# A fused encoder block on one core: row squares, row scaling, output casts and weight casts queued behind the newest operation of their engine, and token tiles requested earlier

## The chip, the cores and the metric

The kernel runs on one core of a Trainium2 chip. Five engines of that core work side by side, each on its own list of instructions in order: TensorE (PE in the profile) multiplies, VectorE (DVE) does two-input elementwise work, ScalarE (ACT) does copies, squares, exponentials and scaling, GpSimd (POOL) does powers and issues some transfers, and SyncE (SP) issues most transfers between the device memory and the on-chip memory. An instruction that needs another engine's result waits for it, and everything behind it on the same engine waits too.

The metric is the device time of one execution in microseconds (us), lower is better. The kernel before takes 2262.73 us, the median of three runs (2262.56, 2262.73 and 2266.06).

## The reference

One transformer layer over 16 meta tokens and 2048 tokens of width 1024, all in float32: a shared input projection, grouped-query attention with 4 query heads and 2 key/value heads, a Fourier mixing of the other half of the channels, an output projection, and an MLP with squared ReLU.

```python
def reference(x, meta_tokens, g_mix, w_in, g_q, g_k, w_fourier, g_attn_out, g_fourier_out, w_out,
              g_mlp, w_up, w_down, g_final):
    h = concat([meta_tokens, x], axis=1)                      # 2064 rows of 1024
    proj = rms_norm(h, g_mix) @ w_in
    q, k, v, u = split(proj)                                  # 512, 256, 256, 512 columns
    q = axial_rope(rms_norm(q, g_q)); k = axial_rope(rms_norm(k, g_k))
    attn = softmax(q k^T / sqrt(128)) v                       # 4 heads of 128, 2 kv heads
    four = real(fft2(u over tokens and 128 channels)) @ w_fourier
    h = h + concat([rms_norm(attn, g_attn_out), rms_norm(four, g_fourier_out)]) @ w_out
    m = rms_norm(h, g_mlp)
    h = h + square(relu(m @ w_up)) @ w_down
    return rms_norm(h, g_final)[:, 16:]
```

## The kernel before

A float32 product is made of three matmuls (`mm3`, lines L81 to L83): each operand is split into a high part, which ACT casts (L71, or L74 with a scale), and a low part, which DVE subtracts (L72, or L75 with a scale). The words "cast" and "low part" below mean these two.

**Stages.** Up to about 230 us the tokens are normalised, transposed and projected, in eight steps j of 256 tokens. Then come the Fourier stage and its output projection, and beside them the attention, which goes on to about 1000 us. The attention's own output projection (`out_a`) and the transposing of its rows (`flip`) run beside the last attention units. From about 1042 us to the end TensorE multiplies for the MLP.

**Tokens.** `load_x(j)` asks on SP for the two tiles x_j_0 and x_j_1 (128 rows of 1024); the tag "x" has three buffers. `prep(j)` squares and sums each row (L249, names jk), has POOL raise the mean to the power -1/2 (L194, names rs_x), scales the row (L254), transposes it on TensorE (L294, names pt), splits it into hth and htl, and stores both parts to ht_d on SP (L304). At its end it asks for both tiles of step j + 1. Projections of q, k and v follow (names pq, pkv), and transposes of q (ptq, L452).

**Weights.** `weight_parts` (L469 to L478) loads eight blocks of w_out (names wf), casts them with a scale (L74 and L75) and stores the parts; each block is loaded, and cast one step later, beside the steps of `prep`. The tag "wf" has one buffer, so that a load waits until the block before it has been stored.

**Attention.** Sixteen units u, each of 512 queries (two heads of 256 tokens) against 17 key tiles. TensorE makes scores s, and ACT copies them out of two rotating banks into S (L829); DVE takes a running maximum M (L835 and L824), subtracts a row (L889), ACT takes the exponential (L890), DVE adds to a sum (L896), and TensorE multiplies by v (L898). `finish(u)` copies the unit's output O, waits for a transfer of the inverse sums (rb), 12 steps later multiplies by it (L917), casts it (ohl, L71), stores it, and squares it (L931).

**Rows behind the attention.** For block b (0 to 3) `out_a(b)` works through four tiles t of 128 rows. For each half of a row TensorE makes poa, DVE adds it to the residual (L1122, names h), and ACT squares the half (L1123, names hj). After the second half DVE sums, POOL takes the power (L194, names rs_m), the row is stored, and `scale_row` scales the row tile before (L1134). `flip(b)` scales the last tile and transposes the rows on TensorE (L1146, names pmt), ACT evacuating each with a scale (L1148, names mt). `mix` and `beside` interleave the generators: a step of `out_a`, a step of the block before's `flip`, and then as many attention steps as fall to it.

**What sets the order.** The program text gives each engine a first order, and a scheduler then settles the order of every engine when the program is built. `tc.issue_after(i)` ties the instructions inside its block, those on the engine of i, to stand behind i; `ins_of` takes the instruction out of a call's result. In the kernel before, the multiplication by rb (L917) is tied to the newest sum (`held["sub"]`); the squares, the scaling, the output cast and the weight casts are not tied to anything.

Of the kernel before, what the change touches and what calls it, by code (L numbers as in the profile page):

```python
# [11 lines left out]
F32 = mybir.dt.float32  # L12
# [45 lines left out]
def f32v(ap):  # L58
    return ap.bitcast(F32)


class Split:
# [5 lines left out]
    def __call__(self, hi, lo, src, scale=None):  # L68
        nc = self.nc
        if scale is None:  # L70
            self.high = nc.scalar.copy(hi, src)  # L71
            self.low = nc.vector.tensor_tensor(lo, src, f32v(hi), op=ALU.subtract)  # L72
        else:
            nc.scalar.activation(hi, src, AF.Copy, scale=scale)  # L74
            self.low = nc.vector.scalar_tensor_tensor(lo, src, scale, f32v(hi), op0=ALU.mult, op1=ALU.subtract)  # L75


# [8 lines left out]
def ins_of(x):  # L86
    return getattr(x, "ins", x)
# [49 lines left out]
def encoder_block(ctx: ExitStack, tc: tile.TileContext, x, meta, w_in, w_f,  # L137
# [26 lines left out]

    xs = {}

    def load_x(j):
        rows = META if j == "m" else P
        for a in range(1 if j == "m" else 2):
            t = tp.tile([P, D], F32, name=f"x_{j}_{a}", tag="x", bufs=3)  # L170
            src = meta if j == "m" else x[(2 * j + a) * P:(2 * j + a + 1) * P, :]
            nc.sync.dma_start(t[:rows], src)
            xs[j, a] = t
# [103 lines left out]

    def prep(j):

        if j == 0:  # L280
            norm_first()
        else:
            for a in range(2):
                norm_x(j, a)
        if j == LAST:
            norm_x("m", 0)
        hT[j] = []
        for kk in range(KT // 2):
            yield
            ps = tbank(f"pt_{j}_{kk}")  # L290
            for i in range(2):
                for a in range(2):
                    k = 2 * kk + i
                    nc.tensor.transpose(ps[:, i * 256 + a * P:i * 256 + (a + 1) * P],  # L294
                                        xs[j, a][:, k * P:(k + 1) * P], ident)
            hi, lo = (t2k(f"ht{e}_{j}_{kk}", [P, 2, 256 + (META if j == LAST else 0)]) for e in "hl")
            split(hi[:, :, :256], lo[:, :, :256], ps.rearrange("p (i n) -> p i n", i=2))
            if (j, kk) == (0, 0):
                early["h"], early["l"] = ins_of(split.high), ins_of(split.low)
            hT[j].append((hi, lo))  # L300
            if 0 < j < LAST:
                for e, t in enumerate((hi, lo)):
                    c = slice((j - 1) % 2 * 256, (j - 1) % 2 * 256 + 256)
                    nc.sync.dma_start(ht_d[(j - 1) // 2][:, 2 * kk:2 * kk + 2, e, c], f32v(t))  # L304
        if j == LAST:
            pm = tbank("pt_m", (P, KT, META))
            for k in range(KT):
                nc.tensor.transpose(pm[:, k, :], xs["m", 0][:META, k * P:(k + 1) * P], ident[:META, :META])
            for kk, (hi, lo) in enumerate(hT[j]):
                split(hi[:, :, 256:], lo[:, :, 256:], pm[:, 2 * kk:2 * kk + 2, :])  # L310
        if 0 < j < LAST:
            load_x(j + 1)
        if j == LAST - 1:
            load_x("m")

    def h_op(j, k, sl):
        if j == "m":
# [151 lines left out]
    def weight_parts():  # L469

        for (k, h), dst in wf_d.items():
            t = wpp.tile([P, 2, 512], R32, name=f"wf{k}_{h}", tag="wf")
            raw = f32v(t[:, 1])
            nc.sync.dma_start(raw, w_out[512 + k * P:512 + (k + 1) * P, h * 512:(h + 1) * 512])
            yield
            split(t[:, 0], t[:, 1], raw, c_fo(k))
            nc.sync.dma_start(dst, f32v(t))
            yield  # L478

# [287 lines left out]
    def a_operand(b, heads):  # L767
# [5 lines left out]
                    nc.sync.dma_start(f32v(A[:, e, k]), o_d[b][:, e, k])  # L773
        return AT[b]

    def attention():

        units = [(b0 + qh, g) for i, (b0, n) in enumerate(BLOCKS)
# [3 lines left out]
        def load_q(u):  # L782
# [1 line left out]
            q = ap.tile([P, 2, 2, 256], R32, name=f"q_{u}", tag="q", bufs=2)  # L784
            nc.gpsimd.dma_start(q, q_d[b][:, :, 2 * g:2 * g + 2])
            return q.rearrange("p l h n -> p l (h n)")

        held = {}

        def start(u, q=None):  # L790
            q = load_q(u) if q is None else q
# [70 lines left out]
        def softmax(u, i):  # L862
# [24 lines left out]
            if i % 2 == 0:  # L887
                mb = s["mb"].rearrange("p (o n) -> p o n", o=1).broadcast_to([P, 2, 512])
                nc.vector.tensor_tensor(S, S, mb, op=ALU.subtract)  # L889
                nc.scalar.activation(p, S, AF.Exp, scale=ISQ)  # L890
                return
            v = vt[j // 2]
            if j == 1:
# [6 lines left out]
        def finish(u):  # L900
# [8 lines left out]
            if u < len(l_d):  # L909
                nc.sync.dma_start(l_d[u], rl)  # L910
                rb = ap2.tile([P, 512], F32, name=f"rb_{u}", tag="rb", bufs=1)
                nc.sync.dma_start(rb, l_d[u].rearrange("(o p) a -> o (p a)", o=1).broadcast_to([P, 512]))
                for _ in range(12):
                    yield
                v = O.rearrange("p (a e) -> p a e", a=4)
                with tc.issue_after(held["sub"]):
                    nc.vector.tensor_tensor(v, v, rb.rearrange("p (e a) -> p a e", a=4), op=ALU.mult)  # L917
            else:
                yield
                nc.vector.tensor_tensor(O, O, rows_to_cols(rl, f"l{u}"), op=ALU.mult)  # L920
            c = slice(b % 2 * 256, b % 2 * 256 + 256)
            if u >= len(units) - 2:
                A = a_operand(3, (2, 3))
                split(A[:, 0, 2 * g:2 * g + 2, c], A[:, 1, 2 * g:2 * g + 2, c], O.rearrange("p (h n) -> p h n", h=2))
            else:
                hl = ap2.tile([P, 2, 512], R32, name=f"ohl_{u}", tag="ohl", bufs=1)
                split(hl[:, 0], hl[:, 1], O)
                for e in range(2):
                    nc.sync.dma_start(o_d[b // 2][:, e, 2 * g:2 * g + 2, c],
                                      f32v(hl[:, e]).rearrange("p (h n) -> p h n", h=2))  # L930
# [165 lines left out]
    def out_a(b):  # L1096
# [14 lines left out]
        ra = rstd_of(mp, ss[:, :T], T, 512, "a")  # L1111
        A = a_operand(b, range(NQ))
        MS[b] = ms = []
        for t in range(T):
            ts = slice(t * P, (t + 1) * P)
            sums = mp.tile([P, 2], F32, name=f"hss_{b}_{t}", tag="hss", bufs=8)
            for half in range(2):
                c = slice(half * 512, (half + 1) * 512)
                ps = bank(f"poa_{b}_{half}_{t}")
                for k in range(NQ):  # L1120
                    mm3(nc, ps, (A[:, 0, k, ts], A[:, 1, k, ts]), WO[k, half], k == 0, k == NQ - 1)
                nc.vector.scalar_tensor_tensor(hs[t][:, c], ps, ra[:, t:t + 1], hs[t][:, c], op0=ALU.mult, op1=ALU.add)  # L1122
                nc.scalar.activation(a_tile(f"hj_{b}_{t}_{half}"), hs[t][:, c], AF.Square,  # L1123
                                     accum_out=sums[:, half:half + 1])
                yield
            sm = mp.tile([P, 1], F32, name=f"hsm_{b}_{t}", tag="hsm", bufs=4)
            nc.vector.tensor_tensor(sm, sums[:, 0:1], sums[:, 1:2], op=ALU.add)
            ms.append(rstd_of(mp, sm, 1, D, ("m", "m2")[b % 2]))
            nc.sync.dma_start(h_d[2 * b0 + t], hs[t])
            if t:  # L1130
                scale_row(b, t - 1)

    def scale_row(b, t):
        nc.scalar.activation(H[b][t], H[b][t], AF.Copy, scale=MS[b][t])  # L1134

    def flip(b):

        if b < 2:
            yield
        scale_row(b, 3)  # L1140
        yield
        hs = H.pop(b)
# [672 lines left out]
```

## Time and profile before

| | |
|---|---|
| median of three runs | 2262.73 us |
| the profiled execution | 2263.3 us |
| its span in the trace | 2261.5 us, so 1.8 us lie around the span |
| granted TensorE clock, mean | 0.996 |
| ACT busy | 1171.4 us, 52% of the span |
| POOL busy | 254.4 us, 11% of the span |
| moved by DMA | 408.08 MB, mean 180 GB/s |

A row of the profile names the engine, the source line, the operation, the output tile and the input tiles (without their numbers), the count, the busy time, and in brackets how long the engine sat idle before it and which engine's instruction ended that idle time. A row of times of start and duration belongs to the view in order of time. A row of a stretch "820.00:860.00" gives, for each engine, the busy time and in brackets the instructions, then the granted TensorE clock (1.00 is full speed) and the share of the DMA engines. Matmul durations are modelled and overlap: at full rate a matmul of 512 columns is listed with some 390 ns while one starts every 227 ns or so.

### The profile page before, as it was taken

To read this page: it belongs to the slowest core of one execution; us is meant where nothing else is said; L and a number is where in the kernel's file an instruction comes from. 1 tells how busy PE (TensorE), PEld (TensorE's weight loads), DVE (VectorE), ACT (ScalarE), POOL (GpSimd) and SP (SyncE) were. 2 spreads that over 40 slices of the span, in tenths; PEclk is the share of its full clock that TensorE was granted. 3 is DMA by queue.
4 is the path that set the end of the run, shared out by engine and by line. 5 is a ranking of instruction groups with operands and counts; after the bars stand their busy time and mean duration, and the time that the engine had idled before them with its cause. 6 is when DMAs were issued, how large, how long until landed. Compare 5 with 4: busy or idle time off the path is not lost.

```text
span 2261.5 us, 27682 instructions
## 1 busy us (share of the span) xinstructions
PE 2227.5 (98%) x9890; PEld 1755.5 (78%) x9890; DVE 1688.2 (75%) x2260; ACT 1171.4 (52%) x1991; POOL 254.4 (11%) x301
## 2 busy tenths in 40 slices
PE   9899999999999999999999999999999999999998
PEld 7788867777777666667888888888888888888887
DVE  6555299999888888988667668788765656786795
ACT  6454255556555656667655554334455555543343
POOL 2232200112332112100000020000110000200000
PEclk9999999999999999999999999999999999999999
DMA  7774743445346424456777577445594444954442
GB/s 267 236 235 136 253 134 90 82 116 167 121 146 200 160 75 133 136 202 246 261 240 241 184 275 249 131 131 171 179 370 172 152 151 154 343 177 152 131 138 84
DMA packets 219914, 408.08 MB, mean 180 GB/s; under 512 B 19568, under 2 KB 97776, under 8 KB 218112
## 3 DMA queue, kind: packets, MB, share of 16 engines
q1 hardware_dynamic: 192000, 343.64, 45.3%
q0 software_dynamic: 27632, 62.41, 9.0%
q8 instruction: 78, 1.28, 0.2%
q14 instruction: 60, 0.49, 0.1%
q10 hardware_dynamic: 144, 0.26, 0.0%
HBM read 260.16 MB, written 146.08 MB: 180 GB/s over the span
## 4 chain that ended last, share of the span: by engine, by line
PE 76%; DVE 10%; issue 4%; DMA 3%; ACT 3%; POOL 1%; SPq 0%; POOLq 0%; DVEq 0%; ACTq 0%
PE o L898 6%; PE dx L83 5%; PE dx L82 5%; PE dx L81 5%; PE ux L83 4%; PE ux L81 4%; PE ux L82 4%; PE dy L83 4%; PE dy L82 4%; PE dy L81 4%; PE uy L83 3%; PE uy L81 3%; PE uy L82 3%; PE s L81 2%; PE s L83 2%
## 5 line engine op out<-in xcount | busy, mean ns | idle before, releaser
L71 ACT CAST ah<-a 128x1024 fp32r<-128x1024 f32 x108 | 112.9, 1050 | 261.4 <-PE dx L82 106.4
L898 PE MATMUL o<-S,vn 128*128 128x512 f32 x512 | 243.7, 597 | 0.1
L829 ACT COPY S<-s 128x512 f32<-128x512 f32 x256 | 147.8, 586 | 130.2 <-PE s L83 121.5
L82 PE MATMUL dx<-bl,ah 128*128 128x512 f32 x496 | 192.5, 388 | 0.0
L83 PE MATMUL dx<-bh,al 128*128 128x512 f32 x496 | 192.5, 388 | 0.0
L81 PE MATMUL dx<-bh,ah 128*128 128x512 f32 x496 | 192.5, 388 | 0.0
L83 PE MATMUL ux<-bf,wul 128*128 128x512 f32 x448 | 174.3, 389 | 0.7 <-DVE wul L72 0.7
L81 PE MATMUL ux<-bf,wuh 128*128 128x512 f32 x448 | 174.5, 389 | 0.0
L82 PE MATMUL ux<-bf,wuh 128*128 128x512 f32 x448 | 174.3, 389 | 0.0
L889 DVE TENSOR_TENSOR S<-S,mb 128x1024 f32<-128x1024 f32 x128 | 153.2, 1221 | 19.8 <-ACT mb L860 19.7
L81 PE MATMUL s<-q,kt 128*128 128x512 f32 (+1 forms) x272 | 151.2, 556 | 10.3 <-ACT S L829 8.8
L890 ACT ACTIVATE S<-S 128x1024 f32<-128x1024 f32 x128 | 134.8, 1064 | 47.9 <-DVE S L889 46.7
L72 DVE TENSOR_TENSOR al<-a,ah 128x1024 fp32r<-128x1024 f32 x108 | 131.0, 1219 | 33.3 <-ACT ah L71 33.0
L81 PE MATMUL dy<-bh,ah 128*128 128x512 f32 (+1 forms) x388 | 150.5, 388 | 0.0
L82 PE MATMUL dy<-bl,ah 128*128 128x512 f32 (+1 forms) x388 | 150.5, 388 | 0.0
L83 PE MATMUL dy<-bh,al 128*128 128x512 f32 (+1 forms) x388 | 150.5, 388 | 0.0
L898 PEld LDWEIGHTS o<-S,vn 128*128 128x128 f32 x512 | 93.6, 190 | 69.7 <-issue 58.5
L835 DVE TENSOR_TENSOR M<-M,S 128x1024 f32<-128x1024 f32 x96 | 117.1, 1220 | 17.1 <-ACT S L829 16.2
L81 PE MATMUL uy<-bf,wuh 128*128 128x512 f32 x320 | 124.9, 390 | 2.0 <-ACT wuh L71 2.0
L83 PE MATMUL uy<-bf,wul 128*128 128x512 f32 x320 | 124.7, 390 | 0.8 <-DVE wul L72 0.8
L82 PE MATMUL uy<-bf,wuh 128*128 128x512 f32 x320 | 124.7, 390 | 0.0
L1279 ACT ACTIVATE c<-c 128x512 f32<-128x512 f32 x96 | 60.5, 631 | 122.1 <-DVE c L1327 120.3
(330 smaller groups left out, 5589.0 us busy)
## 6 DMA issues: line engine op xcount, KB each, us to landing
a<-s_d SPq DMA_DIRECT2D x84, 512.0 KB, 3.9
R<-in_w_up_dram SPq DMA_DIRECT2D x32, 1024.0 KB, 5.5
s_d<-s SPq DMA_DIRECT2D x128, 256.0 KB, 2.1
s_d<-c SPq DMA_DIRECT2D x96, 256.0 KB, 2.7
d<-in_w_down_dram SPq DMA_DIRECT2D x48, 512.0 KB, 5.1
f_d<-lf SPq DMA_DIRECT2D x56, 256.0 KB, 3.1
bf<-f_d SPq DMA_DIRECT2D x7, 2048.0 KB, 13.2
hk<-ht_d SPq DMA_DIRECT2D x24, 512.0 KB, 4.9
```

Source lines behind the costliest of these rows:

```text
L71: self.high = nc.scalar.copy(hi, src)
L72: self.low = nc.vector.tensor_tensor(lo, src, f32v(hi), op=ALU.subtract)
L81: nc.tensor.matmul(out, a[0], b[0], start=first, stop=False, skip_group_check=chain)
L82: nc.tensor.matmul(out, a[0], b[1], start=False, stop=False, skip_group_check=chain)
L83: nc.tensor.matmul(out, a[1], b[0], start=False, stop=last, skip_group_check=chain)
L829: nc.scalar.copy(S[:, i % 2], ps)
L835: nc.vector.tensor_tensor(M, M, S, op=ALU.max)
L889: nc.vector.tensor_tensor(S, S, mb, op=ALU.subtract)
L890: nc.scalar.activation(p, S, AF.Exp, scale=ISQ)
L898: nc.tensor.matmul(s["O"], v[:, 2 * j % 4 + e], p[:, e], start=i + e == 1, stop=False)
L1279: nc.scalar.activation(dst, src, AF.Relu)
```

## The change

It has five parts.

1. `load_x` takes the tiles to load. At the start of `prep(j)` it asks for the first tile of step j + 1, and at its end for the second.
2. In `weight_parts` each load stands behind the newest store of ht on SP, and the cast and the low part stand behind the newest cast and the newest low part that went through the helper `split`.
3. In `out_a` the squares of a half, and the sum, the power, the store and the scaling of a row, are put into a list `late`, which is emptied one half later, behind the next half's matmuls (for the last block at once, as before). For blocks 0 to 2 the square and the scaling stand behind the newest exponential (`held["exp"]`).
4. `flip` of blocks 0 and 1 loses its first empty step.
5. In `finish` the multiplication by rb comes after 10 steps in place of 12, and the cast one step later, tied to the newest exponential.

```diff
@@ Split
-            nc.scalar.activation(hi, src, AF.Copy, scale=scale)
+            self.high = nc.scalar.activation(hi, src, AF.Copy, scale=scale)
@@ load_x
-    def load_x(j):
+    def load_x(j, tiles=(0, 1)):
...
-        for a in range(1 if j == "m" else 2):
+        for a in tiles:
@@ prep
+        if 0 < j < LAST:
+            load_x(j + 1, (0,))
...
-                    nc.sync.dma_start(ht_d[(j - 1) // 2][:, 2 * kk:2 * kk + 2, e, c], f32v(t))
+                    early["store"] = ins_of(nc.sync.dma_start(ht_d[(j - 1) // 2][:, 2 * kk:2 * kk + 2, e, c], f32v(t)))
...
-            load_x(j + 1)
+            load_x(j + 1, (1,))
@@ weight_parts
-            nc.sync.dma_start(raw, w_out[512 + k * P:512 + (k + 1) * P, h * 512:(h + 1) * 512])
+            with tc.issue_after(early["store"]):
+                nc.sync.dma_start(raw, w_out[512 + k * P:512 + (k + 1) * P, h * 512:(h + 1) * 512])
             yield
-            split(t[:, 0], t[:, 1], raw, c_fo(k))
+            with tc.issue_after(ins_of(split.high)), tc.issue_after(ins_of(split.low)):
+                split(t[:, 0], t[:, 1], raw, c_fo(k))
@@ softmax
-                nc.scalar.activation(p, S, AF.Exp, scale=ISQ)
+                held["exp"] = ins_of(nc.scalar.activation(p, S, AF.Exp, scale=ISQ))
@@ finish
-                for _ in range(12):
+                for _ in range(10):
                     yield
...
+                yield
...
-                split(hl[:, 0], hl[:, 1], O)
+                with tc.issue_after(held["exp"]):
+                    nc.scalar.copy(hl[:, 0], O)
+                nc.vector.tensor_tensor(hl[:, 1], O, f32v(hl[:, 0]), op=ALU.subtract)
@@ out_a
+        late = []
+
+        def square(t, half, sums):
+            with behind_exp(b):
+                nc.scalar.activation(a_tile(f"hj_{b}_{t}_{half}"), hs[t][:, half * 512:half * 512 + 512], AF.Square,
+                                     accum_out=sums[:, half:half + 1])
+
+        def row_end(t, sums):
+            sm = mp.tile([P, 1], F32, name=f"hsm_{b}_{t}", tag="hsm", bufs=4)
+            nc.vector.tensor_tensor(sm, sums[:, 0:1], sums[:, 1:2], op=ALU.add)
+            ms.append(rstd_of(mp, sm, 1, D, ("m", "m2")[b % 2]))
+            nc.sync.dma_start(h_d[2 * b0 + t], hs[t])
+            if t:
+                scale_row(b, t - 1)
+
+        def flush():
+            while late:
+                f, *args = late.pop(0)
+                f(*args)
...
+                flush()
                 nc.vector.scalar_tensor_tensor(hs[t][:, c], ps, ra[:, t:t + 1], hs[t][:, c], op0=ALU.mult, op1=ALU.add)
-                nc.scalar.activation(a_tile(f"hj_{b}_{t}_{half}"), hs[t][:, c], AF.Square,
-                                     accum_out=sums[:, half:half + 1])
+                late.append((square, t, half, sums))
+                if half:
+                    late.append((row_end, t, sums))
+                if b == 3:
+                    flush()
                 yield
-            sm = mp.tile([P, 1], F32, name=f"hsm_{b}_{t}", tag="hsm", bufs=4)
...
+        flush()
+
+    def behind_exp(b):
+        return tc.issue_after(held["exp"]) if b < 3 else nullcontext()

     def scale_row(b, t):
-        nc.scalar.activation(H[b][t], H[b][t], AF.Copy, scale=MS[b][t])
+        with behind_exp(b):
+            nc.scalar.activation(H[b][t], H[b][t], AF.Copy, scale=MS[b][t])
@@ flip
-        if b < 2:
-            yield
         scale_row(b, 3)
```

What the change moves on the engines is seen in the order of the built programs. The first place is SP in step j = 2, around the load of x_3_1 (names: hth_2_k and htl_2_k are the parts of the tokens of step 2, wf2_0 a block of the output weights, qt_2 transposed queries). Before:

```order
L477 DMA wf_d1_1_139<-wf1_1_1695 128x1024
L474 DMA wf2_0_1847<-in_w_out_dram 128x512
L304 DMA ht_d0_144<-hth_2_2_912 128x2x256
L304 DMA ht_d0_144<-htl_2_2_913 128x2x256
L456 DMA q_d1_106<-qt_2_923 1024x1x128
L304 DMA ht_d0_144<-hth_2_3_932 128x2x256
L304 DMA ht_d0_144<-htl_2_3_933 128x2x256
L172 DMA x_3_1_940<-in_x_dram 128x1024
```

The same place on SP in the changed kernel:

```order
L306 DMA ht_d0_144<-htl_2_1_848 128x2x256
L306 DMA ht_d0_144<-hth_2_2_914 128x2x256
L172 DMA x_3_1_940<-in_x_dram 128x1024
L306 DMA ht_d0_144<-htl_2_2_915 128x2x256
L458 DMA q_d1_106<-qt_2_925 1024x1x128
```

The load of x_3_1 stands behind the store of hth_2_2 in place of the store of htl_2_3, and the store and the load of weight blocks that stood ahead of it are gone from there (they follow in steps 3 to 6).

The second place is ACT around the scaling of row tile h_0_3, at the end of unit 11's exponentials (S_11_n) and among the copies of unit 12's scores (S_12_n). Before:

```order
L829 COPY S_12_10_7359<-s_12_10_7355 128x512
L829 COPY S_12_10_7359<-s_12_11_7363 128x512
L890 ACTIVATE S_11_12_7101<-S_11_12_7101 128x1024
L931 ACTIVATE O_10_7228<-O_10_7228 128x512
L1134 ACTIVATE h_0_3_6792<-h_0_3_6792,rs_m_7399 128x1024
L829 COPY S_12_12_7376<-s_12_12_7372 128x512
L829 COPY S_12_12_7376<-s_12_13_7380 128x512
L890 ACTIVATE S_11_14_7143<-S_11_14_7143 128x1024
```

The same place on ACT in the changed kernel:

```order
L833 COPY S_12_10_7357<-s_12_11_7361 128x512
L1164 ACTIVATE h_0_2_6790<-h_0_2_6790,rs_m_7285 128x1024
L894 ACTIVATE S_11_12_7099<-S_11_12_7099 128x1024
L833 COPY S_12_12_7374<-s_12_12_7370 128x512
L833 COPY S_12_12_7374<-s_12_13_7379 128x512
L894 ACTIVATE S_11_14_7150<-S_11_14_7150 128x1024
L1164 ACTIVATE h_0_3_6792<-h_0_3_6792,rs_m_7408 128x1024
L833 COPY S_12_14_7400<-s_12_14_7396 128x512
```

The scaling of h_0_3 now stands behind two copies and one exponential that stood behind it; the scaling of the tile before, h_0_2, has come to stand where h_0_3 was.

The third place is ACT around the scaling of h_1_0, among the exponentials of unit 12 and the copies of unit 13 (hj_1_1_0 is a square of the next row tile, mt_0_k an evacuation of block 0's transposes). Before:

```order
L829 COPY S_13_6_7588<-s_13_6_7584 128x512
L1134 ACTIVATE h_1_0_7403<-h_1_0_7403,rs_m2_7594 128x1024
L890 ACTIVATE S_12_6_7307<-S_12_6_7307 128x1024
L890 ACTIVATE S_12_8_7326<-S_12_8_7326 128x1024
L890 ACTIVATE S_12_10_7359<-S_12_10_7359 128x1024
L1123 ACTIVATE hj_1_1_0_7612,hss_1_1_7597<-h_1_1_7405 128x512
L1148 ACTIVATE mt_0_0_7619<-pmt_0_0_7614,cols_97 128x512
L829 COPY S_13_6_7588<-s_13_7_7624 128x512
L829 COPY S_13_8_7641<-s_13_8_7637 128x512
```

The same place on ACT in the changed kernel:

```order
L833 COPY S_13_6_7594<-s_13_6_7590 128x512
L894 ACTIVATE S_12_6_7305<-S_12_6_7305 128x1024
L894 ACTIVATE S_12_8_7324<-S_12_8_7324 128x1024
L894 ACTIVATE S_12_10_7357<-S_12_10_7357 128x1024
L1176 ACTIVATE mt_0_1_7625<-pmt_0_1_7620,cols_97 128x512
L833 COPY S_13_6_7594<-s_13_7_7630 128x512
L1125 ACTIVATE hj_1_1_0_7689,hss_1_1_7596<-h_1_1_7414 128x512
L894 ACTIVATE S_12_12_7374<-S_12_12_7374 128x1024
L833 COPY S_13_8_7647<-s_13_8_7643 128x512
L833 COPY S_13_8_7647<-s_13_9_7651 128x512
L1164 ACTIVATE h_1_0_7412<-h_1_0_7412,rs_m2_7616 128x1024
```

The scaling of h_1_0 has gone from ahead of three exponentials and two copies to behind them; the second copy of S_13_6 comes one square earlier.

More of the change, by code (lines that the diff above doesn't have):

```diff
@@ L311, in prep @@
         if 0 < j < LAST:
-            load_x(j + 1)
+            load_x(j + 1, (1,))
         if j == LAST - 1:
-            load_x("m")
+            load_x("m", (0,))
     def h_op(j, k, sl):
@@ L774, in a_operand @@
         return AT[b]
+    held = {}
     def attention():
@@ L786, in load_q @@
             return q.rearrange("p l h n -> p l (h n)")
-        held = {}
         def start(u, q=None):
@@ L1121, in out_a @@
                     mm3(nc, ps, (A[:, 0, k, ts], A[:, 1, k, ts]), WO[k, half], k == 0, k == NQ - 1)
+                flush()
                 nc.vector.scalar_tensor_tensor(hs[t][:, c], ps, ra[:, t:t + 1], hs[t][:, c], op0=ALU.mult, op1=ALU.add)
-                nc.scalar.activation(a_tile(f"hj_{b}_{t}_{half}"), hs[t][:, c], AF.Square,
-                                     accum_out=sums[:, half:half + 1])
-                yield
-            sm = mp.tile([P, 1], F32, name=f"hsm_{b}_{t}", tag="hsm", bufs=4)
[L1127 to L1131, printed above, removed]
+                late.append((square, t, half, sums))
[3 more added lines that the diff above has]
+                    flush()
+                yield
+        flush()
+    def behind_exp(b):
+        return tc.issue_after(held["exp"]) if b < 3 else nullcontext()
     def scale_row(b, t):
-        nc.scalar.activation(H[b][t], H[b][t], AF.Copy, scale=MS[b][t])
+        with behind_exp(b):
+            nc.scalar.activation(H[b][t], H[b][t], AF.Copy, scale=MS[b][t])
     def flip(b):
-        if b < 2:
-            yield
         scale_row(b, 3)
```

## The prediction

> **What bounds the kernel now.** I began with the busy shares of the page, then went to TensorE's own waits, then to stretches of time.
>
> ```profile
> span 2261.5 us, 27682 instructions
> PE 2227.5 (98%) x9890; PEld 1755.5 (78%) x9890; DVE 1688.2 (75%) x2260; ACT 1171.4 (52%) x1991; POOL 254.4 (11%) x301
> PE s L81 <- ACT S L829: 8.8, 6, 2.4
> PE pm_m L843 <- DVE M L824: 3.6, 5, 0.9
> PE pt L294 <- ACT x L254: 2.3, 1, 2.3
> PE ptq L452 <- ACT jk L249: 2.3, 1, 2.3
> PE uy L81 <- ACT wuh L71: 2.0, 1, 2.0
> PE pq L83 <- DVE htl L72: 1.7, 1, 1.7
> PE uy L83 <- DVE wul L72: 0.8, 1, 0.8
> 780.00:820.00 40.00, 38.14 (x144) 25.30 (x143) 36.02 (x42) 23.90 (x40) 4.88 (x3) 1.00 0.19 54
> 900.00:940.00 40.00, 37.37 (x154) 25.64 (x155) 32.74 (x40) 27.39 (x45) 5.30 (x8) 1.00 0.41 136
> 1042.00:2240.00 1198.00, 1196.62 (x5274) 989.27 (x5273) 862.64 (x1042) 578.86 (x806) 44.99 (x77) 1.00 0.57 195
> ```
>
> TensorE is the bound: 2227.5 of 2261.5 us. The change takes no matmul away, so it can save at most TensorE's idle time and what reduced clock follows it. The MLP stretch offers nothing (1196.62 of 1198 busy); everything lies ahead of 1042 us, and the waits above name the places (8.8 us in six waits for score copies, two waits of 2.3 us for a token tile). DVE, at 36.02 of 40 us in 780 to 820, is the next limit there.
>
> **The tokens (part 1).** SP, ACT, TensorE and the clock around the load of x_3_1:
>
> ```profile
> 75.03 0.59 ACT L71 CAST hth<-pt 128x512 fp32r<-128x512 f32 x1
> 78.09 0.35 SPq L474 DMA_DIRECT2D wf<-in_w_out_dram  x1
> 82.31 1.20 SPq L172 DMA_DIRECT2D x<-in_x_dram  x1
> DMA to landing us min/median/max: 3.5/4.7/6.3
> 88.17 0.60 ACT L249 ACTIVATE jk<-x 128x512 f32<-128x512 f32 x1 [3.57 <-DMA x<-in_x_dram]
> 90.62 1.15 ACT L254 ACTIVATE x<-x,rs_x 128x1024 f32<-128x1024 f32 x1 [0.86 <-POOL rs_x L194]
> 88.94 0.55 PE L452 MATMUL ptq<-ident,qn 128*128 128x128 f32 x3 [2.29 <-ACT jk L249]
> 91.82 0.90 PE L294 MATMUL pt<-ident,x 128*128 128x128 f32 x3 [2.33 <-ACT x L254]
> 92.00:95.50 3.50, 3.50 (x12) 2.92 (x13) 1.74 (x4) 1.36 (x5) 1.33 (x1) 0.59 0.46 133
> ```
>
> The load was issued at 82.31, ACT waited 3.57 us for it, and the squares, power and scaling took from 88.17 to 91.77. TensorE stood 2.29 + 2.33 us, and then ran 3.5 us at 0.59 of its clock, another 3.5 × 0.41 = 1.4: 6.0 us in all. In the new order the load stands right behind the store of hth_2_2, whose cast ended at 75.62, and no weight load (held until 78.09 by its buffer) is ahead. Issued at about 76, landed by 82.3 even at the longest 6.3, and scaled 3.6 later at 85.9, the tile is there before TensorE's first idle moment (88.94 − 2.29 = 86.65). Bounds: −6.0 and, if something else is late at once, 0. I take **−6.0**: the margin of 0.7 us holds with the slowest landing. Its cover gone, the price is the 6.0 again. The wait of 1.7 for htl may shrink with the weight cast gone from ACT's path; I count nothing.
>
> **The weight casts (part 2).** They are moved, not removed:
>
> ```profile
> L74 ACT ACTIVATE wf<-wf,cols x8: 722/724/747, 33.7 to 124.9; 128x512 fp32r<-128x512 f32 x8
> L75 DVE SCALAR_TENSOR_TENSOR wf<-wf,cols x8: 742/748/1225, 38.2 to 125.7; 128x512 fp32r<-128x512 f32 x8
> ```
>
> Eight of 0.72 us on ACT and 0.75 on DVE go to steps 3 to 6, the loads on SP behind the ht stores. At worst each delays a cast that TensorE awaits, 8 × 0.75 = +6.0; at best 0, since ACT's other waits there are long. I take +0.5, near the row: in that stage TensorE waited for DVE's token parts just once, 1.7 us.
>
> **Row scaling and squares (part 3).** The power on POOL, ACT and TensorE at three row tiles (h_1_0, h_0_3, h_1_2):
>
> ```profile
> L194 POOL TENSOR_TENSOR rs_m<-ms_m,mhalf x16: 547/1036/4870, 756.6 to 1029.5; 128x1 f32<-128x1 f32 x16
> 853.20 3.73 POOL L194 TENSOR_TENSOR rs_m<-ms_m,mhalf 128x1 f32<-128x1 f32 x1 [4.60 <-DVE ms_m L192]
> 853.03 3.48 DVE L889 TENSOR_TENSOR S<-S,mb 128x1024 f32<-128x1024 f32 x3
> 856.96 1.15 ACT L1134 ACTIVATE h<-h,rs_m 128x1024 f32<-128x1024 f32 x1 [3.28 <-POOL rs_m L194]
> 862.04 1.05 ACT L829 COPY S<-s 128x512 f32<-128x512 f32 x2
> 862.66 0.65 PE L81 MATMUL s<-q,kt 128*128 128x512 f32 x1 [2.42 <-ACT S L829]
> 862.50:866.00 3.50, 3.34 (x6) 2.02 (x7) 3.36 (x3) 2.14 (x4) 0.00 (x0) 0.55 0.20 75
> 827.79 0.50 PE L81 MATMUL s<-q,kt 128*128 128x512 f32 x1 [2.02 <-ACT S L829]
> 831.00:835.00 4.00, 4.00 (x11) 3.12 (x10) 2.09 (x3) 1.25 (x2) 1.76 (x1) 0.50 0.00 0
> 901.71 0.50 PE L81 MATMUL s<-q,kt 128*128 128x512 f32 x1 [2.08 <-ACT S L829]
> ```
>
> A power over 128 numbers takes 0.55 us at best and 3.73 here, just while DVE ran three two-input subtractions without a break (853.03 to 856.51). ACT stood 3.28 us in front of the scaling; the copies behind it came at 862.04, and TensorE, with two score banks, stood 2.42. In the new order the three exponentials and the copies go ahead of this scaling: the copy at 862.04 moves up by the 3.28 waited and the 1.15 of scaling, to about 857.6 plus waits, before TensorE wants the bank at 860.24 (862.66 − 2.42). For h_0_3 and h_1_2 the order gives the same. What goes: idle 2.42 + 2.02 + 2.08 = 6.5, about 1.1 more from the smaller waits of the 8.8, and the reduced clock, 3.5 × 0.45 = 1.6 at 862 and at least 4.0 × 0.50 = 2.0 at 831: 11.2 in all. Bounds: −11.2 and, if the wait only takes another place, 0. I take **−9.5**: h_0_3 is now two instructions behind its power, and h_1_3 gets its square later.
>
> Rule against row: the Trainium skill, "TensorE: Matmul & The Clock Gate", section "Why this matters for your kernels", sets the limit at idle gaps over some 3 us. By it the gaps here would leave the clock alone, and the sum would lack 1.4 + 1.6 + 2.0 = 5.0 us. The trace disagrees: half clock came behind 2.02 us at 827.79 and none behind 2.08 at 901.71 (1.00 in 900 to 940).
>
> **The rest (parts 4 and 5, and the start of the MLP).** Before the MLP TensorE waits for a cast:
>
> ```profile
> 1033.89 1.04 ACT L71 CAST wuh<-us 128x1024 fp32r<-128x1024 f32 x1
> 1034.98 0.50 PE L81 MATMUL uy<-bf,wuh 128*128 128x512 f32 x1 [2.01 <-ACT wuh L71]
> L917 DVE TENSOR_TENSOR O<-O,rb x15: 1064/1083/1339, 346.0 to 983.2; 128x512 f32<-128x512 f32 x15
> L71 ACT CAST ohl<-O x14: 597/620/632, 347.1 to 950.1; 128x512 fp32r<-128x512 f32 x14
> L1123 ACT ACTIVATE hj<-h x32: 612/632/636, 752.3 to 1025.8; 128x512 f32<-128x512 f32 x32
> ```
>
> In the new order this cast stands one cast earlier on ACT: −1.04, and −1.0 is taken (bounds −2.8, both waits, and 0). The multiplication of outputs moves up by a DVE instruction or two and the ohl casts, 0.62 each, in front of an exponential. In 14 units they cost at worst 14 × 0.62 = +8.7, at best nothing: TensorE has matmuls of v and of two score banks meanwhile. Squares tied to exponentials cost +0.6 where DVE is late. Together +1.0, near nothing since 14 such casts stood there before too.
>
> TensorE coming 2 us earlier at each healed row also reaches DVE's running maximum sooner (3.6 us in five waits now). Bounds 0 and the 6.5 of idle regained; I take +2.5, a good third, since DVE is 82 to 90% busy in these stretches.
>
> **Sum:** −6.0 + 0.5 − 9.5 − 1.0 + 1.0 + 2.5 = −12.5. The profiled execution took 2263.3 (span 2261.5 and 1.8 around it), 0.6 above the median 2262.7, so 2250.8, or **2250** against the median.
>
> **Rivals.**
>
> *The power is still waited for (half of part 3 comes back).* DVE keeps running two-input work next to the power, 3.73 us and up to 4.87, so a scaling behind the newest exponential may still come too soon, and DVE may bind where copies come earlier. For: 36.02 of 40 us of DVE; against: the scaling now comes a half row later. Price +5: 2255. The Trainium skill, "GPSIMD Engine Reference", section "Key points", says that GpSimd shares its path to the memory with DVE instructions of two inputs; the row at 853.20 agrees, and the rule would let the power stay slow wherever it is put.
>
> *Only the tokens gain.* The squares and scalings, now tied, stand in front of other copies, and TensorE stalls elsewhere by as much: −12.5 + 9.5 = −3.0, so 2259.7, within the resolution. For: ACT's list has no gaps to spare when DVE is late; against: the order rows, where copies go ahead.
>
> *Slower.* One mechanism: a tied square or scaling waits on ACT, at the head of its list, for DVE or for the power, and score copies stand behind it. Twelve rows are tied, three stall badly now. A stall costs 2.0 to 2.4 of idle and about 1.8 of clock, say 4. Without part 3's gain the sum stands at −3.0; slower by 0.2% (+4.5) needs 7.5 more, two further rows of the nine that do not stall now: 2267 to 2275. For: three of the four slow powers would still be slow; against: these scalings come later than before.
>
> *The token load does not help,* because the store ahead of it or another input is late: −6.5, 2256.
>
> **How the numbers follow.** A measurement of this kernel tells about 0.2%, 4.5 us, from no change: faster is below 2258.2, slower above 2267.3. Forecast (2243 to 2254) 0.50, power still waited for 0.19, token load no help 0.06: faster 0.75. Only the tokens, with the upper ends of others: 0.16 same. Slower mechanism 0.09. The low end, 2241, is all gains in full (6.0 + 11.2 + 2.8 = 20.0) with little given back; the high end, 2261, takes in the tokens-only case.
>
> **What would show it.** Right: no wait of TensorE for x or jk at 86 to 92 us, and the granted clock in 50 to 100 us at 1.00; x_3_1 issued near 76; TensorE's waits for score copies at 2 us or less in place of 8.8; ACT's wait in front of row scalings well under 3 us each; the clock 1.00 from 820 to 900. Waits for the running maximum of up to 6 us are the give-back. Wrong: new TensorE waits for S, pmt or o with a square or a scaling at the head of ACT's list, or for token parts at 100 to 230 us, where the weight casts now are; then parts 3 or 2 failed.

## The result and the profile after

The changed kernel takes 2238.47 us, the median of four runs (2237.24 to 2240.86), against 2263.73 for the kernel before in the four runs that stand beside it: a ratio of 0.9888, 95% interval 0.9871 to 0.9906. So it is 1.1% faster, and the gain of 25 us is twice the 12.5 that were forecast: the time lies below the low end of the range. The profiled execution took 2238.61 us, its span 2236.8, which is 24.7 below the span before.

The page and, of TensorE's waits in the changed kernel, those that the argument needs (waiting tile and line, what it waited for, us in total, times, longest):

```profile
span 2236.8 us, 27657 instructions
PE 2219.1 (99%) x9890; PEld 1750.8 (78%) x9890; DVE 1686.1 (75%) x2260; ACT 1172.1 (52%) x1991; POOL 260.9 (12%) x301
PE pm_m L847 <- DVE M L828: 2.3, 4, 1.0
PE s L81 <- DMA kt<-k_d: 1.4, 1, 1.4
PE s L81 <- ACT S L833: 0.8, 1, 0.8
PE pq L83 <- DVE htl L72: 0.2, 1, 0.2
```

The two waits of 2.3 us for a token tile are gone, the wait for score copies is 0.8 us where it was 8.8, and the wait for the running maximum, which was to grow, has shrunk from 3.6 to 2.3.

Where the time went is read from instructions that both traces have. In each pair the first row is of the kernel before, the second of the changed one, from the view in order of time (start, duration, engine, line, operation):

```profile
143.19 0.38 PE L452 MATMUL ptq<-ident,qn 128*128 128x128 f32 x2
134.99 0.38 PE L454 MATMUL ptq<-ident,qn 128*128 128x128 f32 x2
206.08 0.38 PE L294 MATMUL pt<-ident,x 128*128 128x128 f32 x2
199.47 0.38 PE L296 MATMUL pt<-ident,x 128*128 128x128 f32 x2
550.75 0.63 PE L843 MATMUL pm_m<-ident,M 128*128 128x128 f32 x4 [0.78 <-DVE M L824]
545.09 0.63 PE L847 MATMUL pm_m<-ident,M 128*128 128x128 f32 x4 [1.04 <-DVE M L828]
927.64 0.50 PE L1107 MATMUL pas<-ones,sq 128*128 128x1 f32 x4
905.83 0.39 PE L1114 MATMUL pas<-ones,sq 128*128 128x1 f32 x3
1010.74 0.50 PE L81 MATMUL uy<-bf,wuh 128*128 128x512 f32 x1 [1.22 <-ACT wuh L71]
```

The last of them stood at 1034.98 before. The lead of the changed kernel at these marks is 8.20, 6.61, 5.66, 21.81 and 24.24 us. So the token stage brings 8.2, 1.6 is lost again where the weight casts now are, the middle of the kernel takes 1.0, the rows behind the attention bring 16.2, and the start of the MLP 2.4. This is one pair of traces. In the five other traces that have parts 1 and 2 the first lead is 8.0 to 8.4 us, and 0.4 to 1.3 of it is lost by the second mark; five traces that have the early stage of before stand 0.5 to 1.3 us behind the kernel before at the first mark, so a mark is good to about 1 us.

The rows by stretches, with the clock, before (the first four rows; two more stand in the prediction) and after (the last six):

```profile
740.00:780.00 40.00, 39.46 (x152) 26.55 (x152) 34.68 (x46) 26.31 (x44) 4.49 (x7) 1.00 0.57 196
820.00:860.00 40.00, 37.98 (x138) 25.61 (x136) 29.57 (x40) 21.23 (x34) 10.80 (x6) 0.91 0.33 97
860.00:900.00 40.00, 37.20 (x140) 24.74 (x139) 35.37 (x43) 24.48 (x43) 7.71 (x6) 0.96 0.48 149
940.00:980.00 40.00, 39.06 (x143) 24.15 (x142) 36.50 (x45) 24.80 (x38) 2.81 (x2) 1.00 0.28 89
740.00:780.00 40.00, 40.00 (x154) 27.24 (x153) 35.74 (x44) 24.17 (x41) 10.94 (x6) 1.00 0.50 170
780.00:820.00 40.00, 39.97 (x154) 26.75 (x153) 37.74 (x48) 26.77 (x44) 6.15 (x4) 1.00 0.28 86
820.00:860.00 40.00, 39.98 (x157) 26.64 (x156) 36.50 (x45) 29.00 (x48) 8.57 (x7) 1.00 0.44 126
860.00:900.00 40.00, 40.00 (x162) 27.68 (x161) 37.09 (x46) 27.62 (x45) 9.67 (x8) 1.00 0.42 135
900.00:940.00 40.00, 40.00 (x160) 27.02 (x159) 35.81 (x43) 25.67 (x40) 10.00 (x5) 1.00 0.43 145
940.00:980.00 40.00, 39.29 (x165) 25.71 (x164) 33.94 (x50) 25.92 (x40) 2.63 (x4) 1.00 0.42 138
```

TensorE is busy almost without a break in the changed kernel, and its clock is 1.00 where it was 0.91 and 0.96. DVE is busier than before (36.50 of 40 us against 29.57) and holds TensorE up by 0.64 us at one place among the rows.

The powers themselves did not get shorter. The sixteen row powers of the changed kernel, the slowest one, and ACT's wait in front of scalings, before (the third row) and after:

```profile
L194 POOL TENSOR_TENSOR rs_m<-ms_m,mhalf x16: 544/1013/8089, 750.9 to 1007.0; 128x1 f32<-128x1 f32 x16
772.11 8.09 POOL L194 TENSOR_TENSOR rs_m<-ms_m,mhalf 128x1 f32<-128x1 f32 x1 [16.96 <-DVE ms_m L192]
ACT h L1134 <- POOL rs_m L194: 17.3, 7, 3.7
ACT h L1164 <- POOL rs_m L194: 2.0, 2, 1.7
```

The longest is 8.09 us now (4.87 before), but ACT stood 2.0 us in front of scalings in place of 17.3. In the new order the power has time to be slow.

### The profile page after: what moved, and what is told of

It is laid out like the page before. It is cut to its first block, busy times and chain, and to the rows that moved or that the text cites. A ratio compares the mean times of both kernels' runs of the same rounds, so it can differ in the third digit from the quotient of the medians.

```text
span 2236.8 us, 27657 instructions
## 1 busy us (share of the span) xinstructions
PE 2219.1 (99%) x9890; PEld 1750.8 (78%) x9890; DVE 1686.1 (75%) x2260; ACT 1172.1 (52%) x1991; POOL 260.9 (12%) x301
## 4 chain that ended last, share of the span: by engine, by line
PE 45%; DVE 3%; DMA 3%; ACT 2%; issue 1%; SPq 0%; POOLq 0%; POOL 0%; DVEq 0%; ACTq 0%
PE dx L81 5%; PE dx L83 5%; PE dx L82 5%; PE dy L81 4%; PE dy L82 4%; PE dy L83 4%; PE ux L83 4%; PE ux L81 3%; PE ux L82 3%; PE uy L83 3%; PE uy L81 3%; PE uy L82 3%; DMA f_d<-lf 2%; DVE wul L72 1%; ACT wuh L71 1%
```

## The experiments

The runs beside each group have their own runs of the kernel before (medians 2261.94, 2261.77 and 2263.38 us), so ratios are compared, and places in the traces. "The rows" below is what a kernel gains on the kernel before between the marks of 550.75 and 927.64 us, each read from one trace; in the changed kernel it is 16.2 us. "Undone" means that the lines of the diff above are as in the kernel before. In what follows theory P is that of the prediction: the loss among the rows is the scaling's wait for the power at the head of ACT's list.

**One part at a time, added to the kernel before.** First the tokens and the weight casts, all else undone:

```diff
+        if 0 < j < LAST:
+            load_x(j + 1, (0,))
...
+            with tc.issue_after(early["store"]):
...
+            with tc.issue_after(ins_of(split.high)), tc.issue_after(ins_of(split.low)):
```

> The kernel before with the token loads and the weight casts of the change alone (parts 1 and 2). Every theory takes the gain ahead of 250 us from here and nothing after it: the traces of before and after stand 8.2 us apart at 150 us and 6.6 at 250 us, so 2263.7 - 6.6 = 2257, with TensorE waiting for no x or jk between 80 and 95 us and all row waits of 740 to 980 us unchanged (s for S copies near 8.8 us). If the prediction's sizes hold instead, -5.5, so 2258. If the lateness at 740 to 980 us had come from the early stage, more than 10 us would go.

Measured: 2252.67 us, ratio 0.9958 (0.9942 to 0.9975), which is 9.3 us below its own runs of before and more than the 6.6 that the marks gave. The mark at 143 us shows the same lead as the changed kernel (8.3 us), and the waits of the rows are all there (s for S copies 8.2 us).

Then part 3 alone, `late`, `square`, `row_end` and `flush` with `behind_exp` on squares and scalings:

```diff
+                flush()
                 nc.vector.scalar_tensor_tensor(hs[t][:, c], ps, ra[:, t:t + 1], hs[t][:, c], op0=ALU.mult, op1=ALU.add)
...
+                late.append((square, t, half, sums))
...
+        with behind_exp(b):
+            nc.scalar.activation(H[b][t], H[b][t], AF.Copy, scale=MS[b][t])
```

> The kernel before with part 3 alone: squares and row ends one half later, squares and scalings behind the newest exponential. Theory P (as predicted, only the wait of the scalings for the power is saved, and DVE takes some of it back): -7 to -9.5, so 2254 to 2257. Theory S (the squares, which waited for DVE in front of score copies, cost as much again): -15 to -17, so 2247 to 2249, with next to no TensorE wait for S copies from 740 to 980 us. Theory E (the rest of the stage's 16 us comes from parts 4 and 5): at most -9, so 2255 or more.

Measured: 2252.60 us, ratio 0.9957 (0.9941 to 0.9973): the forecast's figure for this part, but by luck. The rows bring 16.5 us, about as in the changed kernel, and at the start of the MLP about 5 are lost. The last row's power, and TensorE behind it:

```profile
1013.91 8.21 POOL L194 TENSOR_TENSOR rs_m<-ms_m,mhalf 128x1 f32<-128x1 f32 x1 [6.21 <-DVE ms_m L192]
1023.35 1.12 PE L1171 MATMUL pmt<-ident,h 128*128 128x128 f32 x4 [2.76 <-ACT h L1159]
1023.00:1029.00 6.00, 5.65 (x26) 4.98 (x26) 1.46 (x2) 5.44 (x9) 0.00 (x0) 0.57 0.53 197
```

A power of 8.2 us fell ahead of the last scaling, in block 3, which is tied to nothing; TensorE stood 2.76 us and then ran at 0.57 of its clock.

Then part 3 without the tie of the scalings, and part 3 with that tie alone:

```diff
# squares only: scale_row
-        with behind_exp(b):
-            nc.scalar.activation(H[b][t], H[b][t], AF.Copy, scale=MS[b][t])
+        nc.scalar.activation(H[b][t], H[b][t], AF.Copy, scale=MS[b][t])
# scalings only: out_a
-                late.append((square, t, half, sums))
+                square(t, half, sums)
                 yield
+            row_end(t, sums)
```

> Part 3 with the squares later and behind the newest exponential, the scalings not tied to anything. Theory P: the scalings still wait for the power in front of copies, so little goes, 0 to -3: 2261 to 2264. Theory S: the squares' share, -5 to -8: 2256 to 2259, ACT's wait of hj for h falling from 19 us to under 6.

> Part 3 with the scalings behind the newest exponential only, the squares where they were. Theory P: nearly all of part 3's gain, -8 to -9.5 of idle and clock, so 2254 to 2256, ACT's wait for rs_m from 17 us to under 4. Theory S: the squares' waits (19 us of ACT for h) stay and with them part of the stalls, so -8 to -10 too, but the squares-only and the scalings-only kernels then add up to the 15 to 17 us of both; by P they don't, since the squares bring nothing.

Measured: squares only 2267.59 us, ratio 1.0026 (1.0016 to 1.0035), slower; scalings only 2249.73, ratio 0.9942 (0.9923 to 0.9961), more than either theory gave it. The tie of the scalings alone brings all of the rows, 16.3 us, with powers of up to 10.13 us. Theory S falls: the two do not add up, and later squares by themselves gain nothing. In the squares-only kernel the power comes later while the scaling does not, so ACT stands longer in front of it than the 17.3 us of the kernel before:

```profile
ACT h L1159 <- POOL rs_m L194: 31.4, 10, 4.9
PE s L81 <- ACT S L831: 8.4, 7, 2.7
PE pm_m L845 <- DVE M L826: 5.9, 7, 2.2
1029.83 8.21 POOL L194 TENSOR_TENSOR rs_m<-ms_m,mhalf 128x1 f32<-128x1 f32 x1 [6.20 <-DVE ms_m L192]
1039.27 1.11 PE L1171 MATMUL pmt<-ident,h 128*128 128x128 f32 x4 [3.63 <-ACT h L1159]
```

The stalls among the rows are as long as before, but this trace does not put the slowdown there: its rows are even 4.2 us better, with as much idle time of TensorE and no half clock. It loses 2.2 us from 930 to 990, 4.3 at the start of the MLP, behind another power of 8.2 us ahead of the last scaling (the last two rows), and 1.7 at 1221 us, in a wait for ACT. Whether the other executions lose at the same places is not shown.

**The cause by itself.** The kernel before, and the changed one, without the powers of the rows, each engine's order otherwise unchanged, as the traces show:

```diff
-    def rstd_of(pool, ss, n, width, tag, rows=P):
+    def rstd_of(pool, ss, n, width, tag, rows=P, power=True):
...
+        if not power:
+            return ms
...
-            ms.append(rstd_of(mp, sm, 1, D, ("m", "m2")[b % 2]))
+            ms.append(rstd_of(mp, sm, 1, D, ("m", "m2")[b % 2], power=False))
```

> The kernel before without the 16 powers of the row scalings (it leaves that power out: rows are scaled by their mean square itself); every engine's order is that of before. Theory P (the slow power at the head of ACT's list is the whole loss of the stage): 14 to 17 us go between 740 and 980 us, so 2245 to 2248, TensorE's wait for S copies from 8.8 us to under 2, and the squares' waits for h (19 us of ACT) do no harm by themselves. Theory Q (the scaling and the squares hurt by where they stand, whatever they wait for): half of it at most, 2254 or more.

> The changed kernel without the same 16 powers (left out as in the run before this one), order unchanged. Theory P: the change already hides them, so 0 to -2 us: 2236 to 2239. If powers up to 8 us long still cost the changed kernel something at the start of the MLP or elsewhere, -3 or more.

Measured: 2247.34 us, ratio 0.9936 (0.9920 to 0.9952), and 2239.44, ratio 0.9896 (0.9880 to 0.9913), the same as the changed kernel. In the order of before, without the power:

```profile
PE s L81 <- ACT S L831: 1.2, 2, 0.7
ACT hj L1125 <- DVE h L1124: 19.2, 11, 3.4
820.00:860.00 40.00, 40.00 (x161) 27.54 (x160) 36.81 (x47) 26.48 (x43) 4.85 (x5) 1.00 0.40 112
```

The squares still wait 19.2 us for DVE in front of copies and TensorE does not notice. The rows bring 15.6 us: they are the power's. In the changed kernel nothing of it is left to gain.

Why the power is slow was tried by stopping DVE for it, in the kernel before with a copy added (the helper called for the rows as above):

```diff
         nc.gpsimd.tensor_tensor(rs[:rows], ms[:rows], mhalf[:rows, :n], op=ALU.pow)
+        if not power:
+            held_rs = pool.tile([P, n], F32, name="rh_" + tag, tag="rh_" + tag, bufs=4)
+            nc.vector.tensor_copy(held_rs, rs)
+            return held_rs
```

> The kernel before, with a copy of each row's power on DVE (128 numbers) ahead of the scaling: DVE stops there, one instruction or none behind the mean, until the power is done. Theory C (the power is slow while DVE runs two-input work without a break): no power above 2.5 us (one instruction of 1.2 us, a wait and 0.55), TensorE's wait for S copies under 2 us, and 8 to 14 us gained net of some 0.5 to 1 us of DVE at each of 16 rows: 2248 to 2254. Theory N (the power is slow for another reason): powers of 3 to 5 us stay, DVE stands as long, and the kernel is slower than before: 2265 or more.

Measured: 2250.14 us, ratio 0.9945 (0.9930 to 0.9961), in theory C's range. The powers and TensorE's waits, in the slowest of its four runs (2256.56 us):

```profile
L194 POOL TENSOR_TENSOR rs_m<-ms_m,mhalf x16: 547/1396/2601, 760.6 to 1021.3; 128x1 f32<-128x1 f32 x16
PE s L81 <- ACT S L833: 1.6, 2, 0.9
PE pm_m L847 <- DVE M L828: 3.4, 7, 0.8
```

No power is longer than 2.6 us once DVE stops behind it, which speaks for theory C. The gain in time is not the stop's alone: with the copy added the scheduler settled ACT's order anew, so that one to four ACT instructions now stand between seven of the powers and their scalings where none or one stood. TensorE waits for DVE's maximum seven times in place of five, but 3.4 us in all against 3.6, so no price of the stop is seen there.

**One part at a time, taken out of the changed kernel.** The flip's empty step put back, and the finish as before:

```diff
# flip
+        if b < 2:
+            yield
         scale_row(b, 3)
# finish
-                for _ in range(10):
+                for _ in range(12):
                     yield
...
-                yield
...
-                with tc.issue_after(held["exp"]):
-                    nc.scalar.copy(hl[:, 0], O)
-                nc.vector.tensor_tensor(hl[:, 1], O, f32v(hl[:, 0]), op=ALU.subtract)
+                split(hl[:, 0], hl[:, 1], O)
```

> The changed kernel with the empty first step of flip put back (part 4 undone). Theory F (part 4 keeps the transposes of the last rows ahead of the MLP, and the 5.9 us that rows-only lost at 1020 to 1040 us come back without it): +4 to +6, 2243 to 2245. Theory L (that loss came from one power of 8.2 us that fell among two-input work of DVE, by its moment): within 2 us of 2238.5 with the last power under 2 us, or +5 only if that power is long again.

> The changed kernel with part 5 undone (12 steps ahead of the multiplication by rb, the output cast not tied). The prediction's +1.0 for the rest would give 2237.5, slightly faster without it. Theory L: within 2 us of 2238.5 up to 980 us, and at the start of the MLP +5 only with a long last power. Theory E (the parts beside 3 bring the rest of the gain): +3 or more, spread over 740 to 980 us.

Measured: 2241.25 us, ratio 0.9905 (0.9890 to 0.9920), and 2242.28, ratio 0.9911 (0.9897 to 0.9926). Both intervals overlap that of the changed kernel, so 3 and 4 us are not told apart from nothing by the times. In the traces the rows gain as much as in the changed kernel (16.2 us in both); what differs lies at the start of the MLP:

```profile
1011.13 0.50 PE L81 MATMUL uy<-bf,wuh 128*128 128x512 f32 x1 [2.72 <-ACT wuh L71]
1011.12 0.44 PE L1171 MATMUL pmt<-ident,h 128*128 128x128 f32 x2 [2.87 <-ACT h L1161]
```

The first is of the kernel with the empty step, the second of the one with the old finish; the changed kernel stood 1.22 there. Theory F's 4 to 6 us and theory E's spread gain over 740 to 980 us are not seen. Whether the two parts order that place better, or one execution met it well, stays open.

Then the two halves of the early stage, part 1 and part 2 undone in turn:

```diff
# no early tile: prep
-        if 0 < j < LAST:
-            load_x(j + 1, (0,))
...
-            load_x(j + 1, (1,))
+            load_x(j + 1)
# weights back: weight_parts
-            with tc.issue_after(early["store"]):
-                nc.sync.dma_start(raw, w_out[512 + k * P:512 + (k + 1) * P, h * 512:(h + 1) * 512])
+            nc.sync.dma_start(raw, w_out[512 + k * P:512 + (k + 1) * P, h * 512:(h + 1) * 512])
...
-            with tc.issue_after(ins_of(split.high)), tc.issue_after(ins_of(split.low)):
-                split(t[:, 0], t[:, 1], raw, c_fo(k))
+            split(t[:, 0], t[:, 1], raw, c_fo(k))
```

> The changed kernel with both token tiles asked for at the end of a step again (part 1 undone, part 2 kept). If the weight loads in front of it on SP were what held x_3_1, as the prediction has it, nothing is lost: 2237 to 2241, and x_3_1 still issued before 76 us. If the early request of the first tile is what gains, +6 to +8: 2245 to 2247.

> The changed kernel with the weight loads and casts where they were (part 2 undone, part 1 kept). If the weight loads held x_3_1: the two waits of 2.3 us and the half clock are back at 86 to 95 us, and the 1.3 us lost at 155 to 200 us is not, so +6 to +8 - 1.3: 2243 to 2246. If the early tile gains: 2237 to 2239, less by the 1.3 us.

Measured: 2238.45 us without the early tile, ratio 0.9889 (0.9874 to 0.9903), and 2249.26 with the weights back, ratio 0.9934 (0.9918 to 0.9951). The title's "requested earlier" gains nothing; part 2 gains it all. By the rows below it is the load of a weight block, out of SP's way, that lets the token tile come earlier; but the casts were put back in the same run, so that its time does not tell the two apart. TensorE's wait for htl, which stood behind a weight cast, is 1.9 us again (0.2 in the changed kernel). SP in the changed kernel (first row) and with the weights back, and the clock of the latter:

```profile
73.88 0.45 SPq L172 DMA_DIRECT2D x<-in_x_dram  x1
78.77 0.35 SPq L477 DMA_DIRECT2D wf<-in_w_out_dram  x1
82.97 2.21 SPq L172 DMA_DIRECT2D x<-in_x_dram  x2
50.00:100.00 50.00, 42.77 (x196) 34.53 (x195) 22.42 (x52) 22.90 (x73) 10.31 (x11) 0.93 0.75 240
```

The weights-back kernel also met a wait of 2.6 us for key tiles at 271 us (1.4 in the changed kernel), which is in its 11 us (6 to 8 were expected); that wait differs from trace to trace and no part of the change is near it.

Last, the changed kernel with its squares and row ends at once and only the scalings tied, as in the scalings-only diff above:

> The changed kernel with squares and row ends at once, and only the scalings behind the newest exponential. Theory P (the squares cost nothing where they stood): 740 to 980 us as in the changed kernel, 15 to 16.5 us below before, 2236 to 2241 with 1 to 3 us either way at the start of the MLP. Theory S (squares later are worth 5 us): 2243 or more.

Measured: 2242.03 us, ratio 0.9904 (0.9889 to 0.9918), between the two theories. The rows bring 12.4 us in place of 16.2, and one new stall of size stands among them:

```profile
828.97 0.41 PE L847 MATMUL pm_m<-ident,M 128*128 128x128 f32 x2 [1.83 <-DVE M L828]
```

So with parts 4 and 5 in place the later squares seem to be worth 3 to 4 us; one trace and this row are all that shows it, since the intervals overlap. In the scalings-only kernel, without those parts, prompt squares cost the rows nothing.

No combination came out below the changed kernel, so none is offered as better.

## Why the prediction was right or wrong

The direction and the mechanisms held, but two steps of the sum failed: the rows were sized at 9.5 us and brought 16.2, and a give-back of 2.5 us to DVE was booked that never came.

- **What bounds it.** Right: TensorE's idle time and clock ahead of 1042 us were the whole field. TensorE's idle time fell by 16.3 of the 24.7 us and its busy time by 8.4 with the same matmuls. The clock accounts for 6.7 of the 8.4 (0.97 over 50 to 100 us, 0.91 and 0.96 over the two stretches of 40 above); the other 1.7 stays open.
- **The tokens, −6.0.** Mechanism right (the weights-back and no-early-tile kernels), though it was booked under part 1 and part 2 alone brings it; size 8.2 by the mark. The load was issued at 73.88, sooner than the 76 assumed, and what was counted at nothing, the wait of 1.7 us for htl behind a weight cast, went down to 0.2.
- **The weight casts, +0.5.** +1.6 between the marks at 143 and 206 us (0.4 to 1.3 in the other traces with these parts), within the bounds of 0 and +6.0. That it is the casts' is not shown: TensorE's idle time there is 0.6 us.
- **Row scaling and squares, −9.5, with −11.2 as its bound.** The mechanism was right, and the no-power kernel shows it alone. The term was mis-sized: 16.2 us. The clock was taken from two short stretches (1.6 and "at least" 2.0), while 820 to 860 us at 0.91 and 860 to 900 at 0.96 are worth 3.6 + 1.6 = 5.2, since the stretch cut off at 835 us had begun at 828.72. And the idle time was taken from the waits for S alone. TensorE's idle time from 740 to 980 us fell from 10.8 to 0.8 us, in the rows shown here and in the prediction; the part not counted was mostly its waits for DVE's running maximum. With the clock that is 15.2; the last 1.0 is in neither.
- **DVE takes back +2.5.** This step failed outright: nothing was taken back. The waits for the maximum were read as DVE's limit, but DVE was itself waiting for the same score copies. Its maximum before and after (count, busy time, mean ns, idle time in front of it and what ended most of that):

```profile
L835 DVE TENSOR_TENSOR M<-M,S 128x1024 f32<-128x1024 f32 x96 | 117.1, 1220 | 17.1 <-ACT S L829 16.2
L839 DVE TENSOR_TENSOR M<-M,S 128x1024 f32<-128x1024 f32 x96 | 117.3, 1222 | 6.9 <-ACT S L833 5.8
```

  With the copies on time, DVE's idle time in front of the maximum fell by 10 us, and TensorE's wait for it fell too. A share of 90% busy said that DVE was near a limit, not that it was one. The rival with half of part 3 given back rested on the same reading, and fell with it; its other ground, that the power stays slow, came true without any cost.
- **The rest, −1.0 and +1.0.** The start of the MLP gained 2.4 and no cost of the output casts is seen. One trace does not tell which part of the 2.4 is the order's: the other kernels with most of these parts stood 0.8 to 2.9 us there.
- **The other rivals.** "Only the tokens gain" is what the tokens-alone kernel took (ratio 0.9958). The slower rival, a scaling that waits for a late power at the head of ACT's list, is seen in the squares-only kernel (ratio 1.0026): it needs the squares late and the scalings not. Its price was put at the rows, though, and the trace has the largest loss at the start of the MLP.
- **The low end.** All gains in full are 20.0, and 2262.7 − 20.0 is 2242.7, so the 2241 of the range lay below its own sum; the measured time lies below both.

With the terms at their measured sizes the forecast's sum is −8.2 + 1.6 − 16.2 − 2.4 = −25.2, with 1.0 lost in the middle and 0.5 gained in the MLP −24.7, the difference of the spans.

## What to carry to other kernels

A short instruction that can be slow belongs far ahead of its consumer, and the consumer behind whatever else its engine has ready: tying the scalings behind the newest exponential hid powers up to 8 us long (10 in the scalings-only kernel) without making one of them shorter. When TensorE waits for two engines in a stage, look whether one of them waits for the other first, before its busy share is booked as the next limit; removing the one wait then pays twice. And price a stall with the clock of the whole stretch behind it, not of one piece.

## What the runs showed of the hardware

The power on GpSimd is slow while DVE runs two-input work on the on-chip memory without a break: it took 8.09 us beside DVE's unbroken run in the changed kernel, 8.21 in the part-3 kernel, and at most 2.60 when DVE stopped for it, against 0.54 at best. In the changed kernel the power of 772.11 ended at 780.20, while DVE ran an instruction that has one of its inputs in the matmul's own memory (poa):

```profile
778.55 1.22 DVE L893 TENSOR_TENSOR S<-S,mb 128x1024 f32<-128x1024 f32 x1
779.69 0.75 DVE L1150 SCALAR_TENSOR_TENSOR h<-poa,rs_a,h 128x512 f32<-128x512 f32 x1
```

So DVE need not be idle for the power to end; it is enough here that its next instruction reads one input elsewhere. This agrees with the Trainium skill, "GPSIMD Engine Reference", section "Key points", which names contention of GpSimd with DVE instructions that have two inputs in SBUF, the on-chip memory.

The other traces show the same. In the twelve kernels that have these powers 62 of them took over 2 us, and 61 ended 0.41 to 0.44 us behind the first break in such a run of DVE: an instruction that reads the matmuls' memory, or a pause of as little as 0.03 us. The one left (3.14 us, in the last kernel above) ended inside a run. So a power that meets such a run lasts, in these traces, as long as the run does.

Half clock behind an idle gap is not decided by the gap's length alone. In the kernel before it followed one of 2.02 us and not one of 2.08; in the squares-only kernel none followed a gap of 2.74 (the last two rows). What decides is where the gap falls. In all fourteen traces the granted clock changes only at moments that lie whole multiples of 3.413 us apart, so that a trace falls into stretches of that length; in the kernel before the clock is 0.50 from 91.44 to 94.85 us, from 828.72 to 835.55 and from 862.85 to 866.27. The gap of 2.02 us (825.77 to 827.79) lay inside one stretch; the gap of 2.08 was cut at 900.40 into 0.78 and 1.30, that of 2.74 at 875.45 into 1.20 and 1.54:

```profile
825.31:828.72 3.41, 1.39 (x7) 0.81 (x6) 0.82 (x2) 2.61 (x4) 0.77 (x1) 1.00 0.06 23
828.72:835.55 6.83, 6.83 (x22) 5.67 (x21) 3.66 (x7) 2.19 (x4) 1.93 (x1) 0.50 0.00 0
900.40:903.81 3.41, 2.10 (x9) 1.76 (x10) 0.69 (x1) 3.41 (x5) 0.16 (x1) 1.00 0.27 77
876.99 0.48 PE L81 MATMUL s<-q,kt 128*96 128x512 f32 x1 [2.74 <-ACT S L831]
879.00:885.00 6.00, 5.74 (x29) 4.01 (x28) 3.97 (x7) 1.95 (x4) 0.83 (x2) 1.00 0.80 235
```

Of all the stretches at full clock in these traces, up to the last matmuls, each one with 1.86 us or more of TensorE's idle time was followed by half clock (18 of them), none with 1.74 or less was, and two of the four in between were. Half clock lasted one to three stretches, 3.41 to 10.24 us, and each costs 1.7 us. A gap of 2 us is therefore best priced as its own length and, when it falls inside one stretch, another 1.7 or 3.4 us.
